# Sums of weight parts in a Strassen-like product: four adds on GpSimd replaced by accumulating transfers from memory

## The chip, the cores and the metric

The kernel runs on one core of a Trainium2 chip. The metric is device time in microseconds, the median of several executions. One execution is also taken with the hardware profiler, and all views below are of that one.

## The reference

One decoder layer on 512 tokens of width 1024, all in float32: a combined projection, two groups of attention heads, an output projection with a residual add, and then the MLP that matters here.

```python
    a = jax.nn.relu(rmsnorm(h, g_mlp_norm[l]) @ w_up[l])
    h = h + (a * a) @ w_down[l]
return rmsnorm(h, g_final)
```

`w_up` is 1024 x 4096 and `w_down` 4096 x 1024.

## The kernel before

Every float32 matrix is split into two parts, `hi` (a cast by ScalarE, line 111) and `lo` (source minus `hi`, by VectorE, line 125), and each product is three matmuls: hi·hi, hi·lo, lo·hi.

The MLP runs in four quarters (`for quarter in range(NQ)`). A quarter has two units of the up product and then the down product in two column halves. A unit `g` computes a block of 512 columns of `w_up` against all tokens by a 2 x 2 block scheme with seven products in place of eight (`PRODUCTS`, in this order: B11, T1, B21, T3, T2, T4, B22). The token side of the seven (`tt`, split once, by `split_t`) is made at the start of the MLP from `hs` by sums on VectorE. The weight side is made anew in each unit by the generator `up_weights(g)`: from four parts of `w_up` of 512 x 256, named by (f, d), it yields seven weights:

- B11: part (0,0); B21: part (0,1); T4: part (1,1)
- T1: `s` = (1,0) + (1,1); T3: `s3` = (0,0) + (1,0)
- T2: `s` + (0,0); B22: `s` + (0,1), each added into the same tile `s` after its split before

The adds are POOL's (line 957), on tiles of 128 x 1024. `load_raw` loads a part through SP's queue into a buffer of the tag `wr` (five of them, shared by the `ur` parts of `w_up` and the `dr` parts of `w_down`); the sums have two buffers of the tag `us`. Each weight is split into a slot of a ring of five (`RING`): two `k`, one `vc`, two `q`. So a weight can be split at most five products ahead of TensorE. The two `q` slots hold `hs` at the start of the MLP, until its last sums and splits are through.

`up_product` (line 983) issues 24 matmuls of 256 columns per product. POOL has other work in a unit: `re` (a square, line 1016) and `snap` (T3 less T1, line 1019), which VectorE needs for c22 (line 1024) and, by way of it, for the activations. A down weight `dw` is used by 24 matmuls of 512 columns.

The order of instructions on each engine is not the program's: a scheduler with a model of its own sets it, engine by engine, and each engine and each queue then works strictly in that order. `first_up` draws the first three weights of unit 0 already during the output projection.

Of the kernel before, what the change touches and what calls it, by code (L numbers as in the profile page):

```python
# [10 lines left out]
F32 = mybir.dt.float32  # L11
R32 = mybir.dt.float32r
AF = mybir.ActivationFunctionType
ALU = mybir.AluOpType
# [3 lines left out]
P = 128  # L18
# [76 lines left out]
def layer(ctx, tc, x, xt, w_in, w_uq, w_ukv, w1k, w2k, w1v, w2v, w_o, w_up, w_down, g_final, consts, vecs, out):  # L95
    nc = tc.nc
# [24 lines left out]
    def split(hi, lo, src, eng=None, scale=None, lo_eng=None):  # L121

        hi_of(eng or nc.scalar, hi, src, scale)
        if scale is None:
            (lo_eng or nc.vector).tensor_tensor(lo, src, hi.bitcast(F32), op=ALU.subtract)  # L125
        else:
            nc.vector.scalar_tensor_tensor(lo, src, scale, hi.bitcast(F32), op0=ALU.mult, op1=ALU.subtract)
# [75 lines left out]
    def whole(gen):  # L203

        while True:
            try:
                next(gen)
            except StopIteration as e:
                return e.value
# [19 lines left out]
    def project(ws, n, t, name, tag, every=KD):  # L229
        o = bank(tag, name)  # L230
        s = slice(t * P, (t + 1) * P)
        for k in range(KD):
            mm3(o[:, :n], xth[:, k, s], xtl[:, k, s], ws[k][0], ws[k][1], k == 0, k == KD - 1)
            if k % every == every - 1 and k < KD - 1:
                yield
        return o
# [163 lines left out]
    with tc.tile_pool(name="p0", side="right", **reuse) as p0:  # L400
# [44 lines left out]
        else:  # L445
            xraw[0] = p0.tile([P, KD, P], F32, tag="xr", name="xr", bufs=XB)
            sync.dma_start(vec, vecs)
            for k in range(KD):
                load_w(C_MLA, "wm", w, (k,), **wm)
                if k % 2 == 0 and k < 2 * START:  # L450
                    n = KD // START
# [13 lines left out]
        for t in range(NT):  # L465
            o = whole(project(w, 416, t, "wm_ps", PM[t]))
# [22 lines left out]
    for ws, name, post in ((wk_, "wk", post_k), (wv_, "wv", post_v)):  # L489
        for t in range(NT):  # L490
            o = whole(project(ws, 256, t, name + "_ps", PK[t]))
# [433 lines left out]
    mh = ctx.enter_context(tc.tile_pool(name="mh", **reuse))  # L925
# [6 lines left out]
    def slot(name):  # L932

        n = m["slot"] = m.get("slot", -1) + 1
        tag, size, bufs = RING[n % len(RING)]
        return nsa.tile([P, size], R32, tag=tag, name=name, bufs=bufs)[:, 0:2048].rearrange("p (a n) -> p a n", a=2)

    def split_w(src, name):
        o = slot(name)
        split(o[:, 0], o[:, 1], src)  # L940
        return o
# [1 line left out]
    def split_t(name, src):  # L943
        split(tt[name][:, 0], tt[name][:, 1], src)

    def load_raw(src, name):
        raw = mh.tile([P, 1024], F32, tag="wr", name=name, bufs=5)
        n = src.shape[1]
        sync.dma_start(raw.rearrange("p (k n) -> p k n", n=n), src.rearrange("(k p) n -> p k n", p=P))
        return raw  # L950

    def up_weights(g):

        c0 = 512 * g
        a = {(f, d): load_raw(w_up[0, 512 * d:512 * d + 512, c0 + 256 * f:c0 + 256 * f + 256], "ur")
             for f, d in ((0, 0), (1, 0), (1, 1), (0, 1))}
        add = lambda o, x, y: nc.gpsimd.tensor_tensor(o, x, y, op=ALU.add)  # L957
        s = mh.tile([P, 1024], F32, tag="us", name="us", bufs=2)
        s3 = mh.tile([P, 1024], F32, tag="us", name="us", bufs=2)
        add(s, a[1, 0], a[1, 1])  # L960
        yield split_w(a[0, 0], "uw")
        yield split_w(s, "uw")
        add(s3, a[0, 0], a[1, 0])
        yield split_w(a[0, 1], "uw")
        yield split_w(s3, "uw")
        add(s, s, a[0, 0])
        yield split_w(s, "uw")
        yield split_w(a[1, 1], "uw")
        add(s, s, a[0, 1])
        yield split_w(s, "uw")  # L970

    SETS = (("C", "C", "F", "W"), ("A", "A", "B", "B"))
# [13 lines left out]
    def ctile(name):  # L986
        return mp.tile([P, T], F32, tag="c", name=name, bufs=7)
# [9 lines left out]
    def up_unit(weights, tags):  # L997
# [36 lines left out]
        return acts  # L1034

    first_up = up_weights(0)
    ready = []
    for c in range(2):
        for t in range(NT):
# [3 lines left out]
            for j in range(4):  # L1043
                k = 4 * c + j
# [47 lines left out]
    def pieces(t):  # L1092

        return [(0, 256), (256, 512)] if t == NT - 1 and TSPLIT else [(0, 512)]

    NQ = 4
    for quarter in range(NQ):
        acts = []
        for u in range(2):
            g = 2 * quarter + u  # L1100
            weights = steps(ready, first_up) if g == 0 else up_weights(g)
            acts.append(up_unit(weights, SETS[u]))
        for c in range(2):
# [14 lines left out]
            def add(t, a=0, b=512, n=0):  # L1118
                cs = slice(512 * c + a, 512 * c + b)
                nc.vector.scalar_tensor_tensor(xs[:, t, cs], accs[t, a][:, a:b], r4[:, t:t + 1], xs[:, t, cs],  # L1120
                                               op0=ALU.mult, op1=ALU.add)
                if quarter == NQ - 1:
                    jf = ctile("jf")
                    at = 4 * t + c + n
                    nc.scalar.activation(jf[:, a:b], xs[:, t, cs], AF.Square, accum_out=fs[:, at:at + 1])
                    pre = fs[:, 4 * t + 3:4 * t + 4]
                    if c == 0:
                        nc.vector.tensor_scalar(pre, fs[:, at:at + 1], D * EPS, None, op0=ALU.add)
                        nc.gpsimd.tensor_tensor(xs[:, t, cs], xs[:, t, cs], gf[:, cs], op=ALU.mult)
                    else:  # L1130
                        if n < len(pieces(t)) - 1:
                            nc.vector.tensor_tensor(pre, pre, fs[:, at:at + 1], op=ALU.add)
                        nc.vector.tensor_tensor(fin[t][:, a:b], xs[:, t, cs], gf[:, cs], op=ALU.mult)

            for n in range(4):
                r0 = 1024 * quarter + 256 * n
                ws.append(split_w(load_raw(w_down[0, r0:r0 + 256, 512 * c:512 * c + 512], "dr"), "dw"))
                if last and n >= 2:
                    continue
                for j in range(2):  # L1140
                    for t in range(NT):
                        for a, b in pieces(t) if last else [(0, 512)]:
                            down(t, n, j, a, b)
# [80 lines left out]
```

## Time and profile before

| | |
|---|---|
| median of 3 executions | 659.97 us (659.93 to 660.59) |
| profiled execution | 660.12 us, span 658.3 us |
| TensorE busy | 635.9 us (97%) |
| VectorE, ScalarE, POOL busy | 440.4, 337.0, 258.3 us |
| granted TensorE clock, mean | 0.991 |
| moved by DMA | 56.53 MB, 26.9% of 16 engines on SP's queue |

The busy times are sums over the span; they overlap. The span is the time from the first to the last instruction, and the device time lies 1.8 us above it. A stage is read from its own stretch of the trace.

### The profile page before, as it was taken

The numbers are of one execution on the slowest core, as the hardware profiler recorded it, in microseconds if no ns is written. First come the engines' busy times: TensorE is split into PE (matmuls) and PEld (weight loads), VectorE is DVE, ScalarE is ACT, GpSimd is POOL, SyncE is SP. The second block draws the span as 40 slices with busy tenths as digits, with TensorE's granted clock in tenths as the row PEclk, the third lists the DMA queues.
The fourth block names the chain that finished last, engine by engine and source line by source line (L and its number), as shares of the span: only waits on it lengthen the run. The fifth ranks groups of instructions, "written<-read, shape, count | busy, mean of one in ns | idle before, by whom it ended". The sixth has DMA issues, their size and how long they took to land.

```text
span 658.3 us, 10955 instructions
## 1 busy us (share of the span) xinstructions
PE 635.9 (97%) x4068; PEld 571.5 (87%) x4068; DVE 440.4 (67%) x907; ACT 337.0 (51%) x700; POOL 258.3 (39%) x300
## 2 busy tenths in 40 slices
PE   7999999999999999999699999999999999999996
PEld 5989999998878988888688889998899988999885
DVE  5767577847698589778799425884259743487425
ACT  5567676858846578655545114452135521355213
POOL 3764402326782049531553315413144331344031
PEclk9999999999999999999799999999999999999999
DMA  6533210105421101063025412155111442124003
GB/s 200 148 105 69 68 50 17 33 5 192 119 75 65 33 1 33 1 192 97 33 96 183 138 32 94 64 167 155 34 65 65 165 140 79 55 75 139 22 1 127
DMA packets 47125, 56.53 MB, mean 86 GB/s; under 512 B 4320, under 2 KB 34784, under 8 KB 47072
## 3 DMA queue, kind: packets, MB, share of 16 engines
q1 hardware_dynamic: 46784, 55.57, 26.9%
q8 instruction: 32, 0.52, 0.3%
q10 hardware_dynamic: 288, 0.26, 0.1%
q14 instruction: 21, 0.17, 0.1%
HBM read 53.72 MB, written 2.10 MB: 85 GB/s over the span
## 4 chain that ended last, share of the span: by engine, by line
PE 79%; DVE 10%; DMA 3%; ACT 3%; issue 2%; POOL 1%; SPq 1%; POOLq 0%; ACTq 0%; DVEq 0%
PE up_ps L983 21%; PE dn_ps L132 9%; PE dn_ps L130 9%; PE dn_ps L131 9%; PE pt_ps L585 2%; DVE uw L125 2%; PE hid_ps L730 2%; PE wo_ps L130 1%; PE wo_ps L132 1%; PE wo_ps L131 1%; PE ot_ps L596 1%; PE s_ps L547 1%; PE pt_ps L692 1%; PE ot_ps L597 1%; PE wq_ps L130 1%
## 5 line engine op out<-in xcount | busy, mean ns | idle before, releaser
L131 PE MATMUL dn_ps<-dw,ah 128*128 128x512 f32 (+1 forms) x264 | 101.9, 386 | 0.0
L132 PE MATMUL dn_ps<-dw,al 128*128 128x512 f32 (+1 forms) x264 | 101.6, 386 | 0.0
L983 PE MATMUL up_ps<-ttT,uw 128*128 128x256 f32 x768 | 96.9, 283 | 4.8 <-ACT uw L111 4.4
L130 PE MATMUL dn_ps<-dw,ah 128*128 128x512 f32 (+1 forms) x264 | 101.4, 386 | 0.0
L983 PEld LDWEIGHTS up_ps<-ttT,uw 128*128 128x128 f32 x768 | 93.5, 190 | 5.9 <-ACT uw L111 4.8
L957 POOL TENSOR_TENSOR us<-us,ur 128x1024 f32<-128x1024 f32 x16 | 48.2, 3010 | 84.3 <-DVE uw L125 76.4
L957 POOL TENSOR_TENSOR us<-ur 128x1024 f32<-128x1024 f32 x16 | 41.6, 2608 | 97.6 <-DMA ur<-in_w_up 48.8
L983 PE MATMUL up_ps<-ttB,uw 128*128 128x256 f32 x576 | 75.5, 285 | 3.1 <-ACT uw L111 2.9
L983 PEld LDWEIGHTS up_ps<-ttB,uw 128*128 128x128 f32 x576 | 72.7, 193 | 4.0 <-ACT uw L111 3.1
L125 DVE TENSOR_TENSOR uw<-us,uw 128x1024 fp32r<-128x1024 f32 x32 | 43.3, 1355 | 46.1 <-ACT uw L111 46.1
L125 DVE TENSOR_TENSOR dw<-dr,dw 128x1024 fp32r<-128x1024 f32 x32 | 44.3, 1385 | 34.2 <-ACT dw L111 34.2
L111 ACT CAST uw<-us 128x1024 fp32r<-128x1024 f32 x32 | 33.6, 1049 | 59.3 <-PE dn_ps L132 40.7
L125 DVE TENSOR_TENSOR uw<-ur,uw 128x1024 fp32r<-128x1024 f32 x24 | 40.8, 1699 | 27.3 <-ACT uw L111 27.3
L131 PEld LDWEIGHTS dn_ps<-dw,ah 128*128 128x128 f32 x264 | 49.6, 188 | 10.6
L132 PEld LDWEIGHTS dn_ps<-dw,al 128*128 128x128 f32 x264 | 49.5, 188 | 10.5
L130 PEld LDWEIGHTS dn_ps<-dw,ah 128*128 128x128 f32 x264 | 49.6, 188 | 10.4
L111 ACT CAST dw<-dr 128x1024 fp32r<-128x1024 f32 x32 | 33.1, 1048 | 38.8 <-PE dn_ps L132 21.9
L111 ACT CAST uw<-ur 128x1024 fp32r<-128x1024 f32 x24 | 25.1, 1047 | 31.1 <-PE dn_ps L132 26.6
L125 DVE TENSOR_TENSOR pl<-pt_ps,ph 128x512 fp32r<-128x512 f32 (+3 forms) x60 | 34.2, 578 | 8.3 <-ACT ph L111 6.9
L560 ACT ACTIVATE pr<-pr,mx 128x256 f32<-128x256 f32 (+3 forms) x64 | 36.0, 565 | 6.6 <-DVE mx L552 4.8
L111 ACT CAST ph<-pt_ps 128x512 fp32r<-128x512 f32 (+3 forms) x60 | 29.7, 499 | 16.0 <-PE pt_ps L585 5.4
L1120 DVE SCALAR_TENSOR_TENSOR xs<-dn_ps,small,xs 128x512 f32<-128x512 f32 (+1 forms) x33 | 23.0, 734 | 19.9 <-PE dn_ps L132 19.9
(324 smaller groups left out, 1541.7 us busy)
## 6 DMA issues: line engine op xcount, KB each, us to landing
ur<-in_w_up SPq DMA_DIRECT2D x32, 512.0 KB, 3.8
dr<-in_w_down SPq DMA_DIRECT2D x32, 512.0 KB, 3.7
wor<-in_w_o SPq DMA_DIRECT2D x16, 256.0 KB, 2.9
wqraw<-in_w_in SPq DMA_DIRECT2D x16, 128.0 KB, 2.2
xs<-in_x SPq DMA_DIRECT2D x4, 512.0 KB, 5.9
wmraw<-in_w_in SPq DMA_DIRECT2D x8, 208.0 KB, 4.8
xr<-in_xt SPq DMA_DIRECT2D x3, 512.0 KB, 3.9
out<-xs SPq DMA_DIRECT2D x6, 256.0 KB, 2.2
```

Source lines behind the costliest of these rows:

```text
L111: nc.scalar.copy(dst, src)
L125: (lo_eng or nc.vector).tensor_tensor(lo, src, hi.bitcast(F32), op=ALU.subtract)
L130: nc.tensor.matmul(o, a_hi, b_hi, start=first, stop=False)
L131: nc.tensor.matmul(o, a_hi, b_lo, start=False, stop=False)
L132: nc.tensor.matmul(o, a_lo, b_hi, start=False, stop=last)
L547: nc.tensor.matmul(S[:, :b - a], qs, ka[:, brg, a:b], start=True, stop=False)
L560: nc.scalar.activation(pr[:, :L], pr[:, :L], AF.Exp, bias=lim, scale=-1.0, accum_out=sums[:, 4 + h:5 + h])
L585: nc.tensor.transpose(b[:, h * P:(h + 1) * P], prs[h][:, j * P:(j + 1) * P], ident)
L730: nc.tensor.matmul(hp[0:96, 0:P], xx[:, 2 * i:2 * i + 16 * 95 + 1:16], w1[:, j, :], start=(i == 0), stop=(i == 15))
L957: add = lambda o, x, y: nc.gpsimd.tensor_tensor(o, x, y, op=ALU.add)
L983: nc.tensor.matmul(oj, v[:, x, k, s], t[:, y, k, :], start=first and j == 0 and k == 0 and n == 0, stop=k == 3 and n == 2, skip_group_chec ...
L1120: nc.vector.scalar_tensor_tensor(xs[:, t, cs], accs[t, a][:, a:b], r4[:, t:t + 1], xs[:, t, cs], op0=ALU.mult, op1=ALU.add)
```

## The change

`s` and `s3` are no longer made by adds on POOL. Each starts as a plain load of part (1,0) into a `us` buffer, and the other parts are added by transfers that POOL issues with `accum_op=ALU.add`: they read the part from memory and add it to what the tile holds. A part that is used alone and in a sum is loaded for each use. A unit then has five loads on SP's queue (four before) and four accumulating transfers on POOL's queue, each of 512 KB. The buffers become three of `wr` and four of `us`, seven in all as before.

```diff
-    def load_raw(src, name):
-        raw = mh.tile([P, 1024], F32, tag="wr", name=name, bufs=5)
+    def load_raw(src, name, tag="wr", bufs=3):
+        raw = mh.tile([P, 1024], F32, tag=tag, name=name, bufs=bufs)
...
-        a = {(f, d): load_raw(w_up[0, 512 * d:512 * d + 512, c0 + 256 * f:c0 + 256 * f + 256], "ur")
-             for f, d in ((0, 0), (1, 0), (1, 1), (0, 1))}
-        add = lambda o, x, y: nc.gpsimd.tensor_tensor(o, x, y, op=ALU.add)
-        s = mh.tile([P, 1024], F32, tag="us", name="us", bufs=2)
-        s3 = mh.tile([P, 1024], F32, tag="us", name="us", bufs=2)
-        add(s, a[1, 0], a[1, 1])
-        yield split_w(a[0, 0], "uw")
+
+        def part(f, d):
+            return w_up[0, 512 * d:512 * d + 512, c0 + 256 * f:c0 + 256 * f + 256]
+
+        def add(o, f, d):
+
+            nc.gpsimd.dma_start(o.rearrange("p (k n) -> p k n", k=4), part(f, d).rearrange("(k p) n -> p k n", p=P),
+                                accum_op=ALU.add)
+
+        s = load_raw(part(1, 0), "us", "us", 4)
+        add(s, 1, 1)
+        a11 = load_raw(part(0, 0), "ur")
+        s3 = load_raw(part(1, 0), "us", "us", 4)
+        add(s3, 0, 0)
+        yield split_w(a11, "uw")
         yield split_w(s, "uw")
-        add(s3, a[0, 0], a[1, 0])
-        yield split_w(a[0, 1], "uw")
+        add(s, 0, 0)
+        yield split_w(load_raw(part(0, 1), "ur"), "uw")
         yield split_w(s3, "uw")
-        add(s, s, a[0, 0])
         yield split_w(s, "uw")
-        yield split_w(a[1, 1], "uw")
-        add(s, s, a[0, 1])
+        add(s, 0, 1)
+        yield split_w(load_raw(part(1, 1), "ur"), "uw")
         yield split_w(s, "uw")
```

The scheduler sets a new order with it. The lines of the changed file lie seven further from there on (983 becomes 990, 1019 becomes 1026); the accumulating transfers are line 961. A tile's number tells its unit here: `us_4289` is `s` and `us_4294` `s3` of unit 0, `us_4711` and `us_4716` those of unit 1, `us_5200` and `us_5205` of unit 2, `us_5441` and `us_5446` of unit 3, `us_5930` and `us_5935` of unit 4, `us_6171` and `us_6176` of unit 5, `us_6660` and `us_6665` of unit 6, `us_6901` and `us_6906` of unit 7.

TensorE at the turn from unit 0 to unit 1, before (`uw_4722` is B11' of unit 1, a prime marking the second unit of a pair; `uw_4885` T4', `uw_4919` B22'; some rows left out between):

```order
L983 MATMUL up_ps_4491<-ttB21_4260,uw_4353 128x256 x24
L983 MATMUL up_ps_4725<-ttB11_4258,uw_4722 128x256 x2
L983 MATMUL up_ps_4579<-ttT3_4261,uw_4576 128x256 x2
L983 MATMUL up_ps_4725<-ttB11_4258,uw_4722 128x256 x22
L983 MATMUL up_ps_4611<-ttT2_4262,uw_4608 128x256 x2
...
L983 MATMUL up_ps_4852<-ttT2_4262,uw_4849 128x256 x23
L983 MATMUL up_ps_4820<-ttT4_4263,uw_4885 128x256 x24
L983 MATMUL up_ps_4755<-ttB22_4264,uw_4919 128x256 x2
```

The same place with the change (`uw_4719` is B11', `uw_4886` T4', `uw_4919` B22'):

```order
L990 MATMUL up_ps_4490<-ttB21_4260,uw_4352 128x256 x24
L990 MATMUL up_ps_4722<-ttB11_4258,uw_4719 128x256 x24
L990 MATMUL up_ps_4578<-ttT3_4261,uw_4575 128x256 x2
L990 MATMUL up_ps_4609<-ttT2_4262,uw_4606 128x256 x2
...
L990 MATMUL up_ps_4850<-ttT2_4262,uw_4847 128x256 x24
L990 MATMUL up_ps_4752<-ttB22_4264,uw_4919 128x256 x2
...
L990 MATMUL up_ps_4752<-ttB22_4264,uw_4919 128x256 x14
L990 MATMUL up_ps_4819<-ttT4_4263,uw_4886 128x256 x24
```

All of B11' now stands ahead of T3, and B22' begins ahead of T4'.

VectorE behind the last `hs` of the start, with the change (`uw_4719` is B11', `uw_4575` T3, `uw_4606` T2, `uw_4678` B22, `uw_4782` B21'; before, the split of B11' stood behind those of ttT3 and ttT2):

```order
L1064 TENSOR_TENSOR hs_4265<-hs_4265,hs_4266 128x4x256
L1066 TENSOR_TENSOR hs_4265<-hs_4266,hs_4265 128x4x256
L125 TENSOR_TENSOR ttB22_4264<-hs_4266,ttB22_4264 128x1024
L125 TENSOR_TENSOR ttT3_4261<-hs_4265,ttT3_4261 128x1024
L1068 TENSOR_TENSOR hs_4266<-hs_4266,hs_4265 128x4x256
L125 TENSOR_TENSOR uw_4719<-ur_4714,uw_4719 128x1024
L125 TENSOR_TENSOR ttT2_4262<-hs_4265,ttT2_4262 128x1024
L1001 TENSOR_TENSOR al_4572<-re_4568,ah_4571 128x512
L125 TENSOR_TENSOR ttT4_4263<-hs_4266,ttT4_4263 128x1024
L125 TENSOR_TENSOR uw_4575<-us_4294,uw_4575 128x1024
L125 TENSOR_TENSOR uw_4606<-us_4289,uw_4606 128x1024
```

B11' has moved ahead of the split of ttT2, at the sixth place of the chain.

POOL in the first two units and at the head of the third, with the change; before, the adds `us<-ur` and `us<-us,ur` stood in these places:

```order
L961 DMA us_4289<-in_w_up 128x4x256
L961 DMA us_5200<-in_w_up 128x4x256
L1026 TENSOR_TENSOR snap_4603<-snap_4603,snap_4542 128x512
L961 DMA us_4711<-in_w_up 128x4x256
L961 DMA us_5205<-in_w_up 128x4x256
L961 DMA us_4711<-in_w_up 128x4x256
...
L961 DMA us_5930<-in_w_up 128x4x256
L1023 TENSOR_TENSOR re_6028<-re_6028 128x512
L961 DMA us_6665<-in_w_up 128x4x256
L1026 TENSOR_TENSOR snap_6063<-snap_6063,snap_5996 128x512
```

The transfers into `us_5205` and `us_6665` belong to a later unit and stand ahead of work of the running one: ahead of the last sum of unit 1, and ahead of `snap` of unit 4.

## Rows read from the trace of the kernel before

**Rows 1.** The page: span, busy time of TensorE, SP's DMA queue.
```profile
span 658.3 us, 10955 instructions
PE 635.9 (97%) x4068; PEld 571.5 (87%) x4068; DVE 440.4 (67%) x907; ACT 337.0 (51%) x700; POOL 258.3 (39%) x300
...
q1 hardware_dynamic: 46784, 55.57, 26.9%
```

**Rows 2.** Table by stretches: length, busy us (instructions) of each engine, clock, DMA share, GB/s.
```profile
311.50:318.40 6.90, 0.53 (x4) 0.32 (x3) 6.90 (x7) 5.38 (x7) 1.52 (x1) 0.75 0.08 26
318.40:323.00 4.60, 4.60 (x26) 4.60 (x27) 3.99 (x4) 1.05 (x1) 1.61 (x1) 0.63 0.00 0
...
451.00:536.00 85.00, 84.86 (x531) 76.49 (x531) 50.67 (x53) 31.24 (x38) 28.85 (x13) 1.00 0.31 100
```

**Rows 3.** Waits of TensorE from 304 to 345: total us, times, longest.
```profile
PE up_ps L983 <- ACT uw L111: 7.3, 3, 3.4
```

**Rows 4.** Timeline of TensorE, units 0 and 1: start, us, instruction, idle before it.
```profile
308.50 3.00 PE L983 MATMUL up_ps<-ttB,uw 128*128 128x256 f32 x24
314.42 0.51 PE L983 MATMUL up_ps<-ttB,uw 128*128 128x256 f32 x2 [2.92 <-ACT uw L111]
318.38 0.80 PE L983 MATMUL up_ps<-ttT,uw 128*128 128x256 f32 x2 [3.45 <-ACT uw L111]
...
350.19 0.40 PE L983 MATMUL up_ps<-ttB,uw 128*128 128x256 f32 x2
```

**Rows 5.** Timeline of VectorE behind the last hs.
```profile
309.50 1.23 DVE L1057 TENSOR_TENSOR hs<-hs 128x1024 f32<-128x1024 f32 x1
310.64 1.22 DVE L1059 TENSOR_TENSOR hs<-hs 128x1024 f32<-128x1024 f32 x1
...
319.44 0.68 DVE L994 TENSOR_TENSOR al<-re,ah 128x512 fp32r<-128x512 f32 x1
320.04 2.35 DVE L125 TENSOR_TENSOR uw<-us,uw 128x1024 fp32r<-128x1024 f32 x2
...
334.05 3.40 DVE L125 TENSOR_TENSOR uw<-ur,uw 128x1024 fp32r<-128x1024 f32 x1
```

**Rows 6.** POOL: its adds, grouped (busy us, mean ns, idle before), and one snap.
```profile
L957 POOL TENSOR_TENSOR us<-us,ur 128x1024 f32<-128x1024 f32 x16 | 48.2, 3010 | 84.3 <-DVE uw L125 76.4 <-issue 7.9
L957 POOL TENSOR_TENSOR us<-ur 128x1024 f32<-128x1024 f32 x16 | 41.6, 2608 | 97.6 <-DMA ur<-in_w_up 48.8 <-DVE uw L125 43.5 <-issue 5.3
...
495.25 1.29 POOL L1019 TENSOR_TENSOR snap<-snap 128x512 f32<-128x512 f32 x1
```

**Rows 7.** Loads of line 949 (issue ns min/median/max; landing us), a small load, landings from 275 to 330.
```profile
L949 SPq DMA_DIRECT2D ur<-in_w_up x32: 367/368/506, 279.4 to 571.8; - x32
...
DMA to landing us min/median/max: 3.6/3.8/9.1
...
vec<-in_vecs SPq DMA_DIRECT2D x1, 94.5 KB, 2.0
...
DMA to landing us min/median/max: 3.6/4.6/9.1
```

**Rows 8.** Casts of us (ns, first and last start); timelines of VectorE and TensorE, units 4 and 5.
```profile
L111 ACT CAST uw<-us x32: 1039/1049/1055, 293.2 to 597.3; 128x1024 fp32r<-128x1024 f32 x32
...
466.83 1.22 DVE L125 TENSOR_TENSOR uw<-us,uw 128x1024 fp32r<-128x1024 f32 x1 [4.39 <-ACT uw L111]
...
483.47 1.23 DVE L125 TENSOR_TENSOR uw<-us,uw 128x1024 fp32r<-128x1024 f32 x1 [0.39 <-ACT uw L111]
...
506.85 1.21 DVE L125 TENSOR_TENSOR uw<-us,uw 128x1024 fp32r<-128x1024 f32 x1
...
482.13 3.04 PE L983 MATMUL up_ps<-ttB,uw 128*128 128x256 f32 x24
485.00 3.25 PE L983 MATMUL up_ps<-ttT,uw 128*128 128x256 f32 x26
...
516.42 0.52 PE L983 MATMUL up_ps<-ttB,uw 128*128 128x256 f32 x3
```

## The prediction

> **What bounds the kernel now.** I read the page's first part first: TensorE is busy 97% of a span of 658.3 us [rows 1]. Then the table by stretches, to see where the other 3% lie after the attention: in the 85 us from 451 to 536, one quarter of the MLP, TensorE is busy 84.86 us at full clock, so a quarter has nothing left to give [rows 2]. Between 311.5 and 318.4 it works 0.53 us of 6.9 [rows 2]. The list of waits says on what: 7.3 us in three waits for ScalarE's casts of `uw`, all between 304 and 345 [rows 3]. The timeline puts two of them, 2.92 and 3.45 us, at 314.42 and 318.38, right behind unit 0's B21 [rows 4]; behind them the granted clock is 0.63, so part of the next 4.6 us runs at the lower of the two levels (1.2 of 2.4 GHz) [rows 2]. The cast waits there for a ring slot that `hs` still holds, and `hs` is freed by a chain on VectorE that runs back to back from 309.50 to 322.39 [rows 5]. So this kernel is a full TensorE with one hole of about 8 us at the start of the MLP. POOL's 32 adds take 48.2 + 41.6 = 89.8 us, all off the path in a quarter [rows 6]. What they cost is seen on VectorE: a `uw` subtraction that runs beside an add takes 3.40 us at 334.05, an undisturbed one 1.22 [rows 5, 8].
>
> Three consequences. Removing adds can give back at most the hole. A longer way to each sum costs nothing until it reaches TensorE. So the question is how long an accumulating transfer takes, from the start of its issue on POOL to landing (L), and how long its issue holds POOL (d).
>
> **L and d, which no row shows.** Below: it reads as much from memory as a plain load, so L is at least the loads' median of 3.8 us [rows 7]. Above: two plain loads in a row plus an issue as long as one add, 3.8 + 3.8 + 3.0 = 10.6 us [rows 6, 7]. Between: even a load of 94.5 KB takes 2.0 us [rows 7]; moving goes at 55.57 MB in 26.9% of 658.3 us = 314 GB/s, so 512 KB take 1.67 us [rows 1]; an accumulation passes the tile's old contents through the same engines as well, 2 x 1.67 = 3.3 us; and POOL has to issue it, at a price between SP's 0.37 [rows 7] and an add's 3.0 over the same elements [rows 6]. That is 5.7 to 8.4; among several transfers in flight the median landing rises from 3.8 to 4.6 [rows 7], 0.8 more, so 6.5 to 9.2. I take L = 8.0, d = 1.7 (the middles; every one of these sums is issued beside other loads). The Trainium skill (DMA: Bandwidth & Descriptors, "Anatomy of one DMA — SWDGE (gpsimd) path") fits 2.0 us + bytes/436 GB/s for a transfer issued from GpSimd, 3.2 us for 512 KB, an estimate, and says nothing on accumulation; by it the sum below would be -2.7 us. The plain loads here, issued by SP, take 3.8, which is already more.
>
> **Part by part.**
> *POOL's adds go.* 89.8 us of POOL, off the path; they uncover VectorE's slowed instructions, 1.22 instead of 3.40, which the chains below use.
>
> *Eight more loads and 32 accumulations.* Per quarter that is ten transfers of 512 KB more plus eight re-readings of a tile, 18 x 1.67 = 30 us of the 16 engines in 85. Their share rises from 0.31 [rows 2] to about 0.66. Not a bound, so nothing is added; landing times are in L.
>
> *Two buffers fewer for `wr`, two more for `us`.* Three `dr` buffers at about 5.5 us of TensorE work per weight hold 16 us against a landing of 3.8 [rows 7]. Nothing. SP's queue now has `us` loads between the `dr` loads, and each waits until its buffer's last sum is split; that counts below.
>
> *First sum.* The first load starts at 279.4 [rows 7], lands about 283.2, the accumulation about 291.2; the cast that reads it starts at 293.2 [rows 8]. Covered by 2 us; if that cover goes, the delay runs down the `hs` chain.
>
> *First unit.* The new order puts all of unit 1's B11' ahead of T3, and its split three places earlier on VectorE. From 309.50, VectorE starts a 1024-wide instruction every 1.14 us [rows 5]: six of them put B11' at 316.3, and ten and one short one (0.6) T2's split at 321.5 (322.39 before, [rows 5]). TensorE then does B11' behind the first hole, at the low clock, and with 2.87 us per product (482.13 to 485.00, [rows 8]) is through T4 at about 330. That hole is about as long as before, and I book its loss as before.
>
> *s in unit 0.* B22's sum can be issued when T2's split ends, 321.5, lands at 321.5 + L, is cast (1.05, [rows 8]) and split (1.2): VectorE is through at 323.7 + L. Behind it stand c22 (0.6) and the B21' split (1.14): 325.5 + L.
>
> *s in unit 1: the place that decides.* On POOL the last sum of unit 1 stands behind unit 2's second prefetched sum (`us_5205`). That one's load waits for unit 0's B22 split, and on SP behind `dr_4985`, which waits for the B21' split. So: 325.5 + L, two issues 0.7, landing 3.8, POOL's issue d, then the sum itself L, a cast 1.05. TensorE's B22' can start at 331.1 + 2L + d. Before, it started at 350.19 [rows 4], but behind T4', which now stands behind it: a fair comparison takes off one product, 347.3. With L = 8.0, d = 1.7 it is 348.8: **+1.5 us**. Without any wait TensorE would be there at about 344.6 (T4's end, 330.3, and five products), so the floor of this term is -2.7.
>
> *Second and third quarter: the same pattern without a hole to hide in.* T2's split ends at 484.70 [rows 8]. B22's sum lands at 484.7 + L, split by 487.0 + L; only then does the load of the next-but-one unit's `us` start (0.4 + 3.8), on which POOL waits (d) ahead of `snap` (1.29, [rows 6]): 492.5 + L + d. VectorE's c22 waits for that, and behind it stand six short and three long instructions (3.6 + 3.4 us) up to T2' split: 499.5 + L + d, where the row before has 508.06 [rows 8]. The last sum lands L later, plus a cast: 500.6 + 2L + d, against TensorE's B22' at 516.42 [rows 8]. With 8.0 and 1.7 it is 518.3: +1.9 each, **+3.8 us**. In the last quarter nothing is prefetched, so 508.1 + L + 1.05 = 517.1, 0.7 late if T2' split does not come earlier; it should, since no add slows VectorE any more. I book nothing. T2's sums have 14 us from 468.05 [rows 8] to the 482.4 of their cast (1.05 ahead of 483.47), more than L.
>
> Sum: +1.5 + 3.8 = +5.3. The profiled execution took 660.12 us, 0.15 over the median of 659.97; it is 1.8 above its span. 660.1 + 5.3 = **665.4 us**.
>
> **The rivals.** A measurement of this kernel can tell 0.2%, 1.3 us, from no change.
> *Faster: the sums are quick.* With L up to 6.5 and d near 0.4 the start gains (331.1 + 13.4 = 344.5, the floor, -2.7) and the quarters lose nothing (514.0 against 516.4): 657.4; 656.0 if the low-clock stretch, 4.6 us at 0.63, also shrinks by the 1.4 us it can. For it: the lower end of L, and the clean VectorE. Against: every loading here is with others in flight. It turns into a loss where 2L + d passes 16.2 (start) and 15.8 (quarters).
> *No change.* At L = 7.2, d = 1.7 (2L + d = 16.1): -0.1 at the start and 0.3 in each of the two quarters, so 660.6.
> *Slower still: each issue also waits for VectorE.* POOL and VectorE hold each other up in these rows (3.40 against 1.22 [rows 5, 8]). If issue and transfer each start one VectorE instruction later (1.2 us), 2L + d grows by 3.6: 3 x 3.6 = 10.8 more, 676. The Trainium skill (SBUF — State Buffer, "Who interferes with whom") has such a lockout for the descriptors that GpSimd writes, under VectorE's two-port modes, and says that tensor_tensor has none, which is most of VectorE's work here. No row here has a transfer issued by POOL, so none shows it.
> *The worst corner.* L = 10.6, d = 3.0: 355.3 at the start (+8.0), 2 x 8.4 in the quarters and 3.3 in the last: 688.
>
> **How the numbers follow.** Forecast (2L + d between 16.6 and 19) 35%, VectorE lockout 11%, worst corner 7%: slower 53%. No change 17%. Faster 30%. The likeliest gives 665.4; its own range, from 16.6 and 19, is 662 to 669. The 8-in-10 range has to hold both signs: 656 (the fast end) to 678 (lockout and a little); the corner and what lies under 656 stay out.
>
> **What would show it.** Right: POOL shows transfers and no L957 adds; between issue and landing about 8 us; idle time of TensorE at B22' of units 1, 3 and 5, ended by ScalarE's cast, one to three us each; VectorE's `uw` subtractions back at 1.22; POOL waiting for a `us` load ahead of `snap`. Wrong: landing under 6.5 us, or no wait at B22' of units 3 and 5; or the extra time sitting on `dr` loads, that is, in the down products; or ahead of 304 us, where the first sum would be late.

## The result, and the profile after

The changed kernel takes **690.98 us** (median of 4 runs, 689.96 to 692.16) against 659.95 us of the kernel before in the same comparison (4 runs, 659.67 to 660.59): ratio 1.047, 95% interval 1.0457 to 1.0483. It is 31 us slower. The direction was forecast; the time lies well above the range of 656 to 678. The profiled execution took 692.16 us, with a span of 690.4, 32.1 more than before.

The page of the changed kernel, its lines on the span, the engines and the DMA queues, which answer to [rows 1]:

```profile
span 690.4 us, 11015 instructions
...
PE 648.4 (94%) x4068; PEld 583.5 (85%) x4068; DVE 425.1 (62%) x907; ACT 336.9 (49%) x700; POOL 207.4 (30%) x300
...
q1 hardware_dynamic: 51008, 59.76, 27.7%
q0 software_dynamic: 16896, 16.78, 16.2%
```

TensorE does the same 4068 matmuls, is busy 12.5 us longer and idle 42.0 us instead of 22.4. So 19.6 us are new waits, and 12.5 us are the same matmuls taking longer at a lower clock (mean granted clock 0.968 instead of 0.991). q0 is the new queue, that of the transfers that POOL issues.

The accumulating transfers by their line: the duration of their issue on POOL in ns (min/median/max), then the time from issue to landing. Below them the waits of TensorE (total us, times, longest), to be held against [rows 3]:

```profile
L961 POOL DMA_DIRECT2D us<-in_w_up x32: 1273/1291/1845, 283.6 to 620.4; - x32
...
DMA to landing us min/median/max: 6.0/7.3/12.8
```

```profile
PE up_ps L990 <- ACT uw L111: 14.1, 4, 5.5
PE up_ps L990 <- ACT snap L1019: 8.9, 7, 2.3
PE up_ps L990 <- DVE uw L125: 4.0, 2, 3.2
```

d is 1.29 us and L has a median of 7.3, both a little under the 1.7 and 8.0 of the prediction. The maximum of L is above the highest bound that it gave (10.6). TensorE now also waits 8.9 us for `snap`, a copy on ScalarE that stood in no term of the sum.

The table by stretches, columns as in [rows 2]:

```profile
400.00:450.00 50.00, 41.17 (x316) 40.04 (x315) 26.04 (x28) 19.91 (x26) 15.04 (x11) 0.92 0.71 154
450.00:499.00 49.00, 49.00 (x227) 40.80 (x226) 23.35 (x28) 11.78 (x13) 1.82 (x2) 0.98 0.51 131
499.00:548.00 49.00, 41.90 (x314) 41.00 (x313) 25.63 (x27) 19.32 (x26) 15.60 (x11) 0.90 0.71 151
```

Most of the loss sits in the up products of the second and third quarter (400 to 450, 499 to 548): TensorE works 41 to 42 us of 49 or 50, and the granted clock is 0.92 and 0.90 where a whole quarter had 1.00 [rows 2]. The down products between (450 to 499) are full, but at 0.98.

One chain of the second quarter shows how. First POOL, units 2 and 3, which make this quarter (start, us, instruction, idle before it and what ended that):

```profile
402.18 1.27 POOL L961 DMA_DIRECT2D us<-in_w_up  x1 [13.71 <-DVE xs L1127]
403.81 1.28 POOL L961 DMA_DIRECT2D us<-in_w_up  x1 [0.36 <-DVE uw L125]
...
418.29 1.32 POOL L961 DMA_DIRECT2D us<-in_w_up  x1 [3.47 <-DVE uw L125]
419.11 1.82 POOL L1026 TENSOR_TENSOR snap<-snap 128x512 f32<-128x512 f32 x1
420.35 1.84 POOL L961 DMA_DIRECT2D us<-in_w_up  x1
430.80 2.58 POOL L961 DMA_DIRECT2D us<-in_w_up  x2 [8.61 <-DVE al L1001]
```

Then, over the same stretch, the casts of `us` on ScalarE that read these sums (B22, T2' and B22'), with the re and snap behind the last; the splits on VectorE that release them (T2, T1' and T2'); and TensorE at B22':

```profile
411.61 1.05 ACT L111 CAST uw<-us 128x1024 fp32r<-128x1024 f32 x1 [4.06 <-DMA us<-in_w_up]
...
427.57 1.04 ACT L111 CAST uw<-us 128x1024 fp32r<-128x1024 f32 x1 [3.52 <-DMA us<-in_w_up]
...
442.64 1.04 ACT L111 CAST uw<-us 128x1024 fp32r<-128x1024 f32 x1 [10.43 <-DMA us<-in_w_up]
443.60 0.59 ACT L1022 ACTIVATE re<-up_ps 128x512 f32<-128x512 f32 x1
...
445.02 0.59 ACT L1019 COPY snap<-up_ps 128x512 f32<-128x512 f32 x1
```

```profile
402.29 1.23 DVE L125 TENSOR_TENSOR uw<-us,uw 128x1024 fp32r<-128x1024 f32 x1 [0.33 <-ACT uw L111]
...
416.94 1.23 DVE L125 TENSOR_TENSOR uw<-us,uw 128x1024 fp32r<-128x1024 f32 x1 [0.44 <-ACT uw L111]
...
428.64 1.22 DVE L125 TENSOR_TENSOR uw<-us,uw 128x1024 fp32r<-128x1024 f32 x1 [1.71 <-ACT uw L111]
```

```profile
443.74 0.80 PE L990 MATMUL up_ps<-ttB,uw 128*128 128x256 f32 x2 [5.48 <-ACT uw L111]
445.66 4.63 PE L990 MATMUL up_ps<-ttT,uw 128*128 128x256 f32 x20 [1.12 <-ACT snap L1019]
```

The issue at 402.18 is a first sum of unit 4, fetched ahead. B22's sum, which TensorE needs next, is issued behind it at 403.81, and its cast starts 8.1 us after T2's split (402.29 + 1.23). T1' is split by 418.17, but T2's sum of unit 3 starts only at 420.35: on POOL it stands behind another first sum of unit 4 (418.29) and `snap`. At 430.80 there are two issues in a row again: a first sum of unit 5, then B22's sum of unit 3, and the cast that waits for that one starts 12.8 us after T2' split (428.64 + 1.22). ScalarE waits 10.43 us ahead of this one cast, with `re` and `snap` behind it. From T2's split to the B22' cast it is 39.1 us. Before, the same way took 28.0 us, from 484.70 [rows 8] to this cast:

```profile
512.69 1.05 ACT L111 CAST uw<-us 128x1024 fp32r<-128x1024 f32 x1 [2.88 <-POOL us L957]
```

### The profile page after: what moved, and what is told of

It is laid out like the page before. It is cut to its first block, busy times and chain, and to the rows that moved or that the text cites. A ratio compares the mean times of both kernels' runs of the same rounds, so it can differ in the third digit from the quotient of the medians.

```text
span 690.4 us, 11015 instructions
## 1 busy us (share of the span) xinstructions
PE 648.4 (94%) x4068; PEld 583.5 (85%) x4068; DVE 425.1 (62%) x907; ACT 336.9 (49%) x700; POOL 207.4 (30%) x300
## 3 DMA queue, kind: packets, MB, share of 16 engines
q0 software_dynamic: 16896, 16.78, 16.2%
## 5 line engine op out<-in xcount | busy, mean ns | idle before, releaser
L961 POOL DMA_DIRECT2D us<-in_w_up x32 | 42.5, 1388 | 214.9 <-DVE uw L125 142.0
L990 PE MATMUL up_ps<-ttT,uw 128*128 128x256 f32 x768 | 102.7, 294 | 4.6 <-ACT snap L1019 4.6
L990 PEld LDWEIGHTS up_ps<-ttT,uw 128*128 128x128 f32 x768 | 99.6, 202 | 5.8 <-ACT snap L1019 5.8
L990 PE MATMUL up_ps<-ttB,uw 128*128 128x256 f32 x576 | 80.2, 295 | 22.4 <-ACT uw L111 14.1
L990 PEld LDWEIGHTS up_ps<-ttB,uw 128*128 128x128 f32 x576 | 76.4, 202 | 24.8 <-ACT uw L111 14.9
L125 DVE TENSOR_TENSOR uw<-us,uw 128x1024 fp32r<-128x1024 f32 x32 | 40.4, 1263 | 87.8 <-ACT uw L111 87.8
L125 DVE TENSOR_TENSOR dw<-dr,dw 128x1024 fp32r<-128x1024 f32 x32 | 41.3, 1290 | 37.5 <-ACT dw L111 37.5
L131 PEld LDWEIGHTS dn_ps<-dw,ah 128*128 128x128 f32 x264 | 49.6, 188 | 10.6
L111 ACT CAST dw<-dr 128x1024 fp32r<-128x1024 f32 x32 | 33.1, 1047 | 50.9 <-PE dn_ps L132 32.8
L125 DVE TENSOR_TENSOR uw<-ur,uw 128x1024 fp32r<-128x1024 f32 x24 | 31.0, 1291 | 22.9 <-ACT uw L111 22.9
L552 DVE CUSTOM_DVE_ANT_0 pr<-s_ps,cst 128x256 f32<-128x256 f32 (+4 forms) x64 | 27.8, 447 | 5.4 <-PE s_ps L548 4.5
```

Of the source, the lines that this page charges most:

```text
L111: nc.scalar.copy(dst, src)
L131: nc.tensor.matmul(o, a_hi, b_lo, start=False, stop=False)
L552: nc.vector.tensor_tensor_reduce(pr[:, k0 - 32:k1 - 32], S[:, k0 - a:k1 - a], mask_for(L)[:, k0 - 32:k1 - 32], 1.0, init, ALU.add, ALU.min ...
L961: nc.gpsimd.dma_start(o.rearrange("p (k n) -> p k n", k=4), part(f, d).rearrange("(k p) n -> p k n", p=P), accum_op=ALU.add)
L990: nc.tensor.matmul(oj, v[:, x, k, s], t[:, y, k, :], start=first and j == 0 and k == 0 and n == 0, stop=k == 3 and n == 2, skip_group_chec ...
```

## The experiments

Theory A: three sums stand one behind the other between T2's split and B22', and transfers for the next units stand and travel in front of them on POOL's queue. Rivals: B, the accumulations are too much traffic or too dear each, whatever their order; C, the loads and buffers that changed along with them.

All runs in one table, from the profiled execution of each: the stretches from POOL's `re` of unit 0 to that of unit 2, 4 and 6, and to the end of the span; and T2's split to the B22' cast ("way", in the quarters that begin with units 2 and 4). Stretches and way are of one execution each; that of nopref2 (673.51 us) was its longest of four, that of extra_behind (670.21) its shortest. Each ratio is to the kernel before in the same comparison, whose median was 659.8 to 660.1.

| run | median us, ratio to before [95%] | u0-u2 | u2-u4 | u4-u6 | u6-end | way |
|---|---|---|---|---|---|---|
| before | 659.95 | 95.1 | 84.7 | 84.6 | 80.4 | 28.0, 28.0 |
| the change | 690.98, 1.047 [1.0457, 1.0483] | 101.3 | 97.4 | 94.8 | 84.9 | 39.1, 38.5 |
| plain | 661.97, 1.0034 [1.0018, 1.0050] | 91.8 | 85.6 | 89.5 | 81.7 | 30.3, 32.8 |
| nopref | 672.88, 1.0191 [1.0163, 1.0220] | 103.5 | 88.0 | 86.0 | 84.0 | 30.0, 29.5 |
| nopref2 | 668.92, 1.0118 [1.0093, 1.0143] | 97.0 | 89.3 | 89.0 | 84.8 | 30.9, 31.1 |
| first | 662.75, 1.0039 [1.0021, 1.0057] | 98.7 | 85.0 | 84.5 | 81.6 | 28.4, 27.9 |
| late | 666.63, 1.0104 [1.0070, 1.0137] | 94.8 | 85.7 | 85.8 | 84.3 | 29.0, 29.2 |
| extra_ahead | 711.12, 1.0777 [1.0761, 1.0793] | 110.7 | 97.7 | 98.4 | 90.5 | 41.6, 42.4 |
| extra_behind | 673.75, 1.0228 [1.0189, 1.0266] | 97.2 | 88.1 | 88.4 | 82.5 | 29.9, 30.1 |
| pooladd43 | 660.20, 1.0003 [0.9994, 1.0012] | 93.4 | 84.3 | 84.2 | 81.8 | 26.9, 26.8 |
| first43 | 657.58, 0.9964 [0.9951, 0.9978] | 93.1 | 84.4 | 84.5 | 81.8 | 27.8, 27.8 |
| best | 656.60, 0.9950 [0.9936, 0.9965] | 92.7 | 84.3 | 84.2 | 82.0 | 27.2, 26.8 |

Above 28 us, what the way grows by is within 2 us of what the quarter grows by, in every row: 39.1 - 28.0 = 11.1 against 12.7, 41.6 - 28.0 = 13.6 against 13.0, 32.8 - 28.0 = 4.8 against 4.9, and at the worst 30.9 - 28.0 = 2.9 against 4.6.

**plain: the same transfers, without the accumulation**

```diff
             nc.gpsimd.dma_start(o.rearrange("p (k n) -> p k n", k=4), part(f, d).rearrange("(k p) n -> p k n", p=P),
-                                accum_op=ALU.add)
+                                )
```

> The 32 transfers that POOL issues write instead of accumulating; all else, the queues' order of loads and sums in the quarters too, stays nearly as in the change. (The sums are left out: the second part overwrites the first.) Theory A, the loss is the three transfers in series from T2's split to B22' (8.1, 7.2 and 11.8 us in the second quarter, with POOL's queue between them): a plain one lands in 4 to 5 us, so the stretch from T2's split to the B22' cast falls from 39.1 us to 25 to 29, where before has 28.0; TensorE's idle time is back at 21 to 26 us, and the time at 658 to 668. Theory B, what costs is that POOL issues them and that the loads are arranged anew (10 loads per unit pair in SP's queue, three wr buffers): 680 to 691, however fast they land.

The transfers by their line (issue on POOL, landing), and their queue on the page:

```profile
L961 POOL DMA_DIRECT2D us<-in_w_up x32: 751/751/974, 282.8 to 592.1; - x32
...
DMA to landing us min/median/max: 4.0/5.0/8.6
```

```profile
q0 software_dynamic: 4608, 16.78, 8.3%
```

661.97 us. The transfers land earlier by 2.0 us (least) to 4.2 (most), the way is 30.3 and 32.8 us, and 29 of the 31 us are gone. So neither that POOL issues the transfers nor the loads' arrangement makes the loss. The stretch u4-u6 still loses 4.9 us: the pattern of three in series with others ahead is there, with a smaller L.

**nopref and nopref2: all 32 accumulations, in another order**

```diff
+        behind = lambda: tc.issue_after(m["last"].ins) if g else contextlib.nullcontext()
+        with behind():
-        add(s, 1, 1)
+            add(s, 1, 1)
...
+        with behind():
-        add(s3, 0, 0)
+            add(s3, 0, 0)
...
-        add(s, 0, 1)
+        m["last"] = add(s, 0, 1)
```

(nopref2 has `if g >= 2` in place of `if g`.)

> The first two sums of each unit are issued only behind the last sum of the unit before, so none stands ahead of, or in flight beside, a sum that TensorE waits for. Theory A: in the second quarter us_5441+00 no longer waits 2.2 us for the prefetch and snap, and us_5441+01 lands in 6 to 8 us instead of 11.8; T2's split to the B22' cast falls from 39.1 to 30 to 33 us, three sums in series still being longer than three adds; TensorE's idle falls by 6 to 12 us and the time to 668 to 678. Unless the first sums, issued later, now come late for T1' (that would show as a wait at T1'). Theory B, the accumulations load the 16 DMA engines whatever their order: 686 to 694.

> All 32 accumulating transfers of the change; only from unit 2 on, a unit's first two sums are issued behind the last sum of the unit before. Unit 1's stay early, as in the change. Theory A (transfers of the next unit standing and travelling in front of the awaited ones): the start loses its 6.2 us too, since unit 2's first sums no longer stand ahead of unit 1's last (re of unit 0 to re of unit 2: 94 to 97 us, 101.3 in the change, 95.1 before, 103.5 with all held), the quarters stay at 86 to 88, so 662 to 668 with the whole traffic of the change. Theory B (the traffic and the price of the packets): not under 673, the value with all held.

nopref: 672.88 us, 18 us of the loss back with the same transfers. The B22 and B22' casts of units 2 and 3 (ScalarE) and POOL's last three-fold issue, where B22's sum now goes first and the next unit's two behind it:

```profile
413.00 1.05 ACT L112 CAST uw<-us 128x1024 fp32r<-128x1024 f32 x1 [2.68 <-DMA us<-in_w_up]
...
436.27 1.05 ACT L112 CAST uw<-us 128x1024 fp32r<-128x1024 f32 x1 [4.28 <-DMA us<-in_w_up]
```

```profile
430.10 3.92 POOL L961 DMA_DIRECT2D us<-in_w_up  x3 [8.38 <-DVE uw L126]
```

The awaited sum's cast starts 6.2 us after its issue (430.10 to 436.27) although two more follow right behind. The way is 30.0 us. Of the 14.6 us that its span is still longer, 8.4 lie in the start (103.5 instead of 95.1): unit 1's first sums, now held, come late. nopref2 lets those two go early, and the start falls to 97.0; its 668.92 us is 0.92 above the upper end of what theory A gave, its quarters of 89 (in its longest execution) are 1 longer, and B's floor of 673 is missed. **Order alone gives back 22 of the 31 us.** Some 9 us are left; late, below, loses 6.8 with the awaited sums alone.

**first and late: half of the sums each**

```diff
 first (us 3, wr 4 buffers)
-        add(s, 0, 0)
+        padd(s, s, a00)
...
-        add(s, 0, 1)
+        padd(s, s, a01)

 late (padd is a POOL tensor_tensor add)
-        s = load_raw(part(1, 0), "us", "us", 4)
-        add(s, 1, 1)
+        a10 = load_raw(part(1, 0), "ur")
+        s = load_raw(part(1, 1), "us", "us", 4)
+        padd(s, s, a10)
...
-        add(s3, 0, 0)
+        padd(s3, a00, a10)
```

> Only the first two sums of a unit (the ones fetched ahead) are made by accumulating transfers; the two in place, which follow a split and are waited for, are POOL adds as before (us 3 and wr 4 buffers). Theory A: no transfer is left in the chain from T2's split to B22', so the quarters are full again: idle of TensorE 18 to 24 us, 655 to 662 us, the lower end if VectorE's subtractions at the start are less slowed. Theory B (traffic and the price of a packet): half of the accumulations are left, so about half of the loss of 31 us, 670 to 678.

> The other half: the two first sums of a unit are POOL adds, the two in place, each behind a split, are accumulating transfers (us 4 and wr 3 buffers). Theory A: all three transfers in series are still there, only without others beside them, 6 to 7.5 us each; T2's split to B22' is 30 to 34 us, and the time 668 to 680, most of the loss from half of the transfers. Theory B: the same time as with the other half, 670 to 678.

first 662.75 (theory A's upper end was 662), late 666.63 (below its lower end of 668). B wanted the same 670 to 678 from both. The losses of the halves, 2.9 and 6.8 us, make 9.7, not 31: neither half holds the cause alone. In late every awaited sum is alone on POOL's queue. TensorE does not wait for it at B22' there, and still loses 1.0 us a quarter; where, is shown in the part on the prediction. The B22 sum's issue (POOL) and cast (ScalarE) in unit 2 of late:

```profile
399.90 1.30 POOL L961 DMA_DIRECT2D us<-in_w_up  x1 [3.59 <-DVE uw L125]
```

```profile
405.99 1.05 ACT L111 CAST uw<-us 128x1024 fp32r<-128x1024 f32 x1 [2.36 <-DMA us<-in_w_up]
```

6.1 us from issue to cast.

**extra_ahead and extra_behind: one useless transfer per unit, on either side of the awaited one**

```diff
 late, with
-        yield split_w(s, "uw")
-        add(s, 0, 1)
+        w2 = split_w(s, "uw")
+        yield w2
+        tiny = glob.tile([P, 1], F32, tag="tiny", name="tiny", bufs=1)
+        mark = nc.gpsimd.tensor_copy(tiny, w2[:, 1, 0:1].bitcast(F32))
+        with tc.issue_after(mark.ins):
+            mark = add(s3, 0, 1)
+        with tc.issue_after(mark.ins):
+            add(s, 0, 1)
 extra_behind: s and s3 exchanged in the two adds
```

> The run with POOL adds for the first sums and accumulating transfers in place, and to each unit one useless accumulation (into s3, after its last use) is added, issued right ahead of B22's sum; both follow T2's split. Nothing else is held up. Theory A1 (the transfers of POOL's queue move one after the other, so the one ahead counts in full): the awaited sum lands 11 to 13 us after its issue instead of 6.2, T2's split to the B22 cast goes from 6.4 to 11 to 13.5 us in every unit, T2's split to the B22' cast from 29 to 38 to 41, a quarter from 85.7 to 94 to 97 us, and the time to 690 to 706: most of the change's loss from 8 transfers that nobody waits for. Theory A2 (two in flight share the engines, whichever was issued first): 8.5 to 10 us, time 675 to 688, and the run with the same transfer behind gives the same.

> The same kernel with the useless accumulation issued right behind B22's sum instead of ahead of it. Theory A1: the awaited sum lands in 6.2 to 7 us as if alone, T2's split to the B22 cast stays at 6.4 to 7.2 us, time 666 to 672 (the run without it: 666.6). Theory A2: 8.5 to 10 us, time 675 to 688, as with the transfer ahead.

`mark` is a small copy on POOL that holds both issues until T2's split is done. 711.12 against 673.75 us: the same transfers, issued in the same 2.6 us, 37 us apart by which of the two goes first. Unit 2 in both, first with the useless one ahead (POOL's two issues, the B22 cast on ScalarE), then with it behind:

```profile
411.03 2.60 POOL L961 DMA_DIRECT2D us<-in_w_up  x2
```

```profile
421.69 1.05 ACT L111 CAST uw<-us 128x1024 fp32r<-128x1024 f32 x1 [6.92 <-DMA us<-in_w_up]
```

```profile
401.66 2.60 POOL L961 DMA_DIRECT2D us<-in_w_up  x2 [0.31 <-issue]
```

```profile
407.75 1.05 ACT L111 CAST uw<-us 128x1024 fp32r<-128x1024 f32 x1 [2.61 <-DMA us<-in_w_up]
```

With the other one behind, the awaited sum is there 6.1 us after the first issue, as alone in late. With it ahead, 10.7. Two in flight do not share the engines evenly; the one behind waits for the one ahead. The Trainium skill (DMA: Bandwidth & Descriptors, "Two DMAs through the same engine are not ordered") says that within one queue of one DMA engine descriptors start in order but are pipelined; these two runs agree, and put 4.6 us on it (10.7 - 6.1), less than a whole transfer's 6.1. Both times lie above what A1 gave (690 to 706 and 666 to 672), by 5 and 2 us. So with a transfer behind the awaited one the kernel is still 7 us slower than late; how much of that is the transfer and how much the copy `mark`, no run separates.

**pooladd43, first43 and best: the buffers alone, and transfers only where nobody waits**

```diff
 pooladd43: part (1, 0) loaded twice into us (4 buffers), wr 3, all sums padd
 first43:   first, with us 4 and wr 3 buffers
 best:      pooladd43, with
+        if g < 2:
+            add(s, 1, 1)
...
+        if g < 2:
+            add(s3, 0, 0)
```

> The loads and buffers of the change (part (1,0) read twice straight into us, us 4, wr 3), but all 32 sums are POOL adds; no transfer is issued by POOL. Theory A: the arrangement of loads and buffers costs little by itself, 658 to 664. Theory C, that these are what makes the change slow: 670 to 691.

> The run with accumulating first sums and POOL adds in place, with us 4 and wr 3 buffers instead of 3 and 4. Unit 1's first sums are now all done ahead of 300 us. Theory A: no accumulation is awaited in the start, so the stretch from re of unit 0 to re of unit 2 falls from 98.7 to 92 to 95 us (91.8 with plain transfers, 95.1 before); the quarters stay at 85.0: 656 to 661. Theory C (buffers): three wr buffers, of which two hold a part until its add, make the dr loads late: waits of TensorE at down products, 662 to 670.

> Accumulating transfers only for the first two sums of units 0 and 1, which are issued long before TensorE needs them; every other sum is a POOL add (us 4, wr 3 buffers). Theory A: start as good as with plain transfers or a little less (92 to 94 us from re to re), quarters at 84.7 to 85.0: 655.5 to 659.5, faster than before by the slowed VectorE instructions of unit 1. Theory C: later loads for want of wr buffers, 660 to 668.

pooladd43 takes the same time as before, so theory C is out. first43 is 5.2 us faster than first by one buffer moved from `wr` to `us`, since unit 1's first sums are then done early. best, 656.60 us, is 0.5% faster than before, clear of noise but small. It differs from pooladd43 in four sums, those of units 0 and 1. Of the 3.6 us between their spans (658.9 and 655.3), 3.1 are there by `re` of unit 0. VectorE of pooladd43 ahead of the `hs` chain, then POOL's adds of the same stretch:

```profile
288.36 2.58 DVE L125 TENSOR_TENSOR ttB<-hs,ttB 128x1024 fp32r<-128x1024 f32 x1 [1.12 <-ACT ttB L111]
...
295.05 2.98 DVE L125 TENSOR_TENSOR uw<-ur,uw 128x1024 fp32r<-128x1024 f32 x1
...
301.54 2.69 DVE L125 TENSOR_TENSOR ttT<-hs,ttT 128x1024 fp32r<-128x1024 f32 x1 [0.52 <-ACT ttT L111]
...
312.30 1.23 DVE L1069 TENSOR_TENSOR hs<-hs 128x1024 f32<-128x1024 f32 x1
```

```profile
287.45 2.41 POOL L965 TENSOR_TENSOR us<-us,ur 128x1024 f32<-128x1024 f32 x1 [0.56 <-DMA us<-in_w_up]
294.55 2.41 POOL L965 TENSOR_TENSOR us<-us,ur 128x1024 f32<-128x1024 f32 x1 [4.69 <-DVE uw L125]
300.74 2.40 POOL L965 TENSOR_TENSOR us<-us,ur 128x1024 f32<-128x1024 f32 x1 [3.79 <-DMA ur<-in_w_up]
```

Each add has a VectorE instruction of 2.6 to 3.0 us beside it, where an undisturbed one takes 1.2. In best one add is left there, and the `hs` chain begins at 309.16:

```profile
297.84 4.15 DVE L125 TENSOR_TENSOR ttT<-hs,ttT 128x1024 fp32r<-128x1024 f32 x1
...
309.16 1.23 DVE L1074 TENSOR_TENSOR hs<-hs 128x1024 f32<-128x1024 f32 x1
```

## Why the prediction was right and wrong

*What bounds the kernel: right.* TensorE was full, a longer way costs only where it reaches it, and the way that reached it is the one named, from T2's split to the cast of B22'. What there was to win is small, as said: best wins 3.5 us in all, most of it ahead of unit 2.

*L and d: right in size, wrong as one number.* d 1.29, L 6.0 to 12.8 with a median of 7.3. The estimate that the prediction worked out from the Trainium skill (DMA: Bandwidth & Descriptors, "Anatomy of one DMA — SWDGE (gpsimd) path"), 3.2 us for 512 KB, is missed by the plain transfers (4.0 at least) and by more by the accumulating ones (6.0 at least).

*The step that failed* is "The last sum lands L later", which put 8.0 us from T2' split to the sum. In the second quarter the cast that waits for it starts 12.8 us after that split, in the third 11.8. A prefetched sum stands right ahead of it on POOL. The prediction had seen prefetched sums on that queue and charged their issue, d, but not their travel. The second quarter piece by piece, against before: T2's split to the B22 cast 8.1 instead of 3.9; on to T1' split 6.6 instead of 9.1; to the T2' cast 9.4 instead of 6.9; to T2' split 2.3 instead of 3.5; to the B22' cast 12.8 instead of 4.6. The last piece is most of it. extra_ahead, with a useless transfer in that place, takes 12.6 us from T2' split to this cast; extra_behind takes 7.0 and late 6.4.

The prediction's formula for the way is 14.8 + 2L + d (from 499.5 + L + d and L more, less 484.7): 32.5 us with its own 8.0 and 1.7, and 30.7 with the measured medians, against 39.1 and 38.5. With late's median L of 6.2 and d of 1.29 it gives 28.5, measured 29.0, but that is luck: late has no prefetched sum ahead of `snap`, which the formula counts, and has the sum of T2' in its chain, which the formula leaves out. In the last quarter nothing is fetched ahead; there the prediction had 508.1 + L, which less 484.7 is 30.7 with the median L, and 30.7 is measured (596.78 to 627.49).

*A sum left out.* "T2's sums have 14 us" was read from the first unit of a pair alone. T2' had only 6.9 us before, from T1' split to its cast. With the change its sum stands behind a prefetched one and `snap`, the cast waits 3.52 us for it, and TensorE then waits 2.07 us at B21' for the `snap` behind that cast.

*The deadline, put some 2.6 us too late.* The prediction held the cast of B22' against TensorE's B22' at 516.42. But TensorE does only three matmuls of B22' there and then turns to T4', which needs the `snap` that stands behind this cast on ScalarE. Before, `snap` and T4':

```profile
516.45 0.58 ACT L1012 COPY snap<-up_ps 128x512 f32<-128x512 f32 x1
```

```profile
517.08 3.12 PE L983 MATMUL up_ps<-ttT,uw 128*128 128x256 f32 x24
```

Between the cast and `snap` stand `re` on ScalarE, its square on POOL and the cast of `ah`. T4' starts 0.05 us after `snap` ends, so the way of 28.0 us had no room at all. The same two in late:

```profile
432.40 0.58 ACT L1023 COPY snap<-up_ps 128x512 f32<-128x512 f32 x1
```

```profile
433.03 3.13 PE L994 MATMUL up_ps<-ttT,uw 128*128 128x256 f32 x24 [1.09 <-ACT snap L1023]
```

From the start of the B22' cast to T4' it is 4.4 us in both (512.69 to 517.08, 428.63 to 433.03). late's way is 1.0 us longer and TensorE waits 1.09 us, where the prediction's comparison would have found room. With this deadline its own L and d would have booked 4.5 us a quarter (32.5 - 28.0) instead of 1.9.

*The rows that could have told.* The order of POOL's queue was at hand: first sums of the next units stand between the awaited ones. What no row of before showed is that transfers of that queue go one after another; the median landing of several loads on SP's queue, 4.6 instead of 3.8 [rows 7], was taken for it, and is no measure of one transfer right behind another. The deadline could be read from before: T4' starts where `snap` ends.

*The start: a hit that hides a miss.* B22' of unit 1 was put at 348.8, and starts at 348.66. But T4' now stands behind, and unit 1 ends 3.6 us later than before (357.7 against 354.1), where +1.5 was booked. Behind the wait of 3.83 us ahead of B22' the granted clock is 0.62 (348.66 to 351.69) and 0.76 (to 354.0), where before it was 1.00. Four down matmuls stand there in both kernels, first with the change, then before:

```profile
349.61 2.07 PE L130 MATMUL dn_ps<-dw,ah 128*128 128x512 f32 x4 [0.44 <-ACT dw L111]
```

```profile
350.42 1.09 PE L130 MATMUL dn_ps<-dw,ah 128*128 128x512 f32 x4
```

The later B22' makes 1.4 of the 3.6 us (348.66 against the 347.3 of the prediction); the rest is what follows it, mostly these slower matmuls. The 348.8 was in part luck, too: POOL issued the sum of B22' 0.3 us after T2' split (340.23), as late as the counted way, by the transfer at 338.86, allowed. T2' split was that late because its sum, issued at 328.87 behind a prefetched one, reached its cast only 9.1 us later, and that way was not counted.

*The last quarter, booked at nothing, costs 4.5 us* (84.9 against 80.4), and 3.9 in late: the way of 30.7 and 29.8 there is longer than 28.0 too. The prediction had found it 0.7 late and then let VectorE's quicker instructions pay for that. With the change TensorE waits 0.76 us at B22' there and 1.65 at T4' for `snap`, and the granted clock is 0.96 (596 to 640).

*The clock, booked at nothing in the quarters*, costs most of 12.5 us of the 32: the waits come in pieces of up to 5.5 us, and with them the granted clock is 0.90 to 0.92 over a stretch of 50.

*Right, at nothing:* the buffers (pooladd43, ratio 1.0003), the DMA share (forecast about 0.66; 0.71 and 0.51 in the two halves of a quarter; nopref2 carries the same transfers 22 us faster), and the first sum (T1's cast at 294.64 instead of 293.17; TensorE comes to it at 304.58 and does not wait). VectorE came back as forecast, but for nothing. Its subtractions of `uw`, mean ns in the fourth number:

```profile
L125 DVE TENSOR_TENSOR uw<-us,uw 128x1024 fp32r<-128x1024 f32 x32 | 40.4, 1263 | 87.8 <-ACT uw L111 87.8
L125 DVE TENSOR_TENSOR uw<-ur,uw 128x1024 fp32r<-128x1024 f32 x24 | 31.0, 1291 | 22.9 <-ACT uw L111 22.9
```

The same two groups had 1355 and 1699 ns before.

*The rivals.* The worst corner gave 688, near the result in its number only: it needed 10.6 us for every transfer, and the median is 7.3. The lockout by VectorE is not seen: issues take 1273 to 1291 ns from the least to the median, with VectorE busy 62% of the span. "Faster: the sums are quick" is half borne out: plain, with 2L + d = 10.8 (5.0 and 0.75) where the rival allowed 13.4, gains at the start (91.8 instead of 95.1) but loses in the quarters (4.9 us in u4-u6), and takes 661.97 us, slower than before. best is faster for another reason: nobody waits for its four transfers.

Open: in extra_behind the way is 29.9, 0.9 above late's 29.0, but its median 7 us above late's. The traces show a part: in its second quarter T4' waits 1.65 us for `snap` instead of 1.09, and the granted clock is 0.98 where late has 1.00. Where the rest lies is open.

## What to carry to other kernels

A transfer put in an engine's place has a latency for each use and a queue for all uses: before counting its latency, list what stands in front of it on that queue when somebody waits for it, and charge each of those its travel (here 4.6 of 6.1 us) and not only its issue. Move what is fetched ahead, and leave on the engine what follows a result and is waited for; here the 16 sums fetched ahead can all be transfers without a loss (first43), four of them bring the gain (best), and the 16 awaited ones make the loss, most of all where others stand ahead of them. An in-order engine that waits for a transfer (ScalarE in its cast) holds back all behind it, so look for the second wait (`snap`) that such a stall makes: the deadline is the first instruction of the full engine that needs anything behind the transfer, and not only the one that reads its result.

## What the runs showed of the hardware

- An accumulating transfer is dearer than a plain one of the same 512 KB in every part: its issue takes POOL 1.29 us instead of 0.75, it lands after 6.0 us at the least instead of 4.0, and it moves in 528 packets instead of 144 (16896 and 4608 by 32), with 16.2% of the engines' span instead of 8.3%.
- Accumulating transfers that POOL issues land one after the other: 10.7 us from the first issue to the awaited cast with another transfer right ahead, 6.1 with it right behind.
- Some kernels with transfers on POOL's queue vary more from run to run, highest less lowest: nopref2 7.6 us, extra_behind 6.8, first 5.6, late 5.0, plain 4.1; before 2.0 in 19 runs. The change itself (2.2) and extra_ahead (1.5) do not. The cause is open.
